# The first output projection's first rows in the joining's free buffer, and the roots behind the first two projections on VectorE

## The chip, the cores and the metric

One core of one Trainium2 chip. The metric is the device time of one launch in microseconds (us), median of several runs; lower is better. The engines are called as the profile calls them: PE (TensorE), DVE (VectorE), ACT (ScalarE), POOL (GpSimd), SP (SyncE, which here only issues transfers).

## What is computed

One decoder layer on a sequence of 2048 rows of 1024 numbers, in float32. `hn` is the row-normed input, `proj` its input projection (q, k, v of an attention group, and the two halves of a gated conv group). What matters here is the middle: the two groups are joined, go through one output projection, and are normed twice.

```python
attn_out = sliding_window_attention(q, k, v, attn_sinks, rel_bias)
conv_out = conformer_conv(u, conv_dw, conv_dw_b, conv_ln_g, conv_ln_b, w_conv_pw)
mixed = jnp.concatenate([attn_out, conv_out], axis=-1) @ w_out
h = h + rms_norm(mixed, mix_post_g)
hn = rms_norm(h, ffn_pre_g)
ff = (jax.nn.silu(hn @ w_gate) * (hn @ w_up)) @ w_down
h = h + rms_norm(ff, ffn_post_g)
```

## The kernel before

The sequence is cut into 4 tiles of 512 rows. Each tile t goes through stages: A (input projection), B (attention), C (31 conv taps on each of four columns of 128 channels, written to `y_scr`, then a tail: load from `y_scr`, transpose, layer norm, swish, store to `mixT`), W (output projection, post norm, residual, second norm). The second norm's rows go to `hn_scr`, from which H transposes them for the feed-forward stages F and G. One extra stage, J, multiplies the conv's pointwise weights into the lower half of `w_out` once (`w_join`), so that the tail's result goes straight into W. H, F and G take two tiles at a time.

Every product is made in three matmuls: each operand is split into a rounded high part and the rest (function `three`, called with PE's line L108). For a row chunk of `mixT` this is `operand`: ACT copies the high part into half of an `hl` tile (L782), DVE subtracts it into the other half (L85 is the line of all DVE arithmetic). For weights it is `split_w` (ACT L133, DVE L85). So a matmul of W waits for: the load of its rows (L804), ACT's copy, DVE's subtraction, and the same for its weights (load L143).

The tags of `t_` name pools of buffers with a fixed count. Those of the change: `wx`, one buffer of 128 x 1024, used by J for its even inputs and by each W for one residual block (L857); `fa`, four of 128 x 512, used by many stages. `mb` is a pool of two, of which one is a spare tile, used by J for its odd inputs and by W1 for its rows.

The order of the work: the code writes a main run of stages (A0 to A3, then W1, F, G) and lanes beside it that get credit with the main run's progress (`run`, `Lane.pump`); W0 runs in a lane beside A3, as do taps, tails and J. From the dependencies and priorities that this gives, a planner sets a fixed order of instructions for each engine before the launch. Each engine then works through its queue in that order and stops at the first instruction whose inputs or buffer are not there; SP's queue of transfers works in the same way.

W0 is `stage_w(0, True, 2, "x", "hl", "fa", mm)`: four groups of two row chunks (gi = 0 to 3); for each, the two halves of 512 output columns, for each half four row blocks, each a chain of 6 matmuls into a `mm` bank. The first group is copied from the bank by ACT (L757), the others are added by DVE. The banks of `mm` are four; A3 and W share them. Behind it stands `norm_w`: squares summed by ACT (L844), a root, scale, residual, squares again (L866), the second root, ACT's scaling of four blocks (L873) and the stores to `hn_scr` (L876).

The root is `rsqrt`: three small DVE instructions for a first guess, then three Newton steps on tiles of 128 x 4. With `beside_taps` a step is four POOL instructions (L159 to L162), without it three DVE instructions:

```python
if beside_taps:
    ptt(t, y, y, ALU.mult)
    ptt(t, t, v, ALU.mult)
    nc.gpsimd.tensor_scalar(t, t, -0.5, 1.5, ALU.mult, ALU.add)
    ptt(y, t, y, ALU.mult)
else:
    vtt(t, y, y, ALU.mult)
    stt(t, v, -0.5, t, ALU.mult, ALU.mult)
    stt(y, t, 1.5, y, ALU.add, ALU.mult)
```

Before, W0, W1 and W2 use POOL, W3 uses DVE.

Of the kernel before, what the change touches and what calls it, by code (L numbers as in the profile page):

```python
# [23 lines left out]
D = 1024  # L24
DFF = 2816
P = 128
T = 512
# [10 lines left out]
def layer_kernel(ctx, tc, x, xT, cols, rows, sinks, relb, onehot, w_in, w_four, w_pw, w_out, w_gate, w_up, w_down, out):  # L38
# [10 lines left out]
    def nm(s):  # L49
        uid[0] += 1  # L50
        return f"{s}@{lab[0]}_{uid[0]}"
# [3 lines left out]
    def t_(tag, shape, dt=F32):  # L55
        return sb.tile(list(shape), dt, tag=tag, name=nm(tag), bufs=BUFS[tag])

    def f4(tag, shape=(P, D)):
        return t_(tag, shape)

    def f2(tag, shape=(P, T)):
        return t_(tag, shape)

    def hl(tag):
        return t_(tag, (P, 2, T), F32R)

    def sm(n, dt=F32):
        kind = "A" if lab[0][0] == "G" else lab[0][0]
        return sb.tile([P, 8], dt, tag="sm" + kind, name=nm("sm"), bufs={"C": 8, "W": 4}.get(kind, 16))[:, 0:n]
# [70 lines left out]
    def weight(src, low, made, raw=None, on_pool=True):  # L140
        if raw is None:
            raw = t_("raw", (P, 2, T))
            nc.sync.dma_start(raw, src)  # L143
        return [split_w(raw[:, n], "w", low[n], made, on_pool) for n in range(2)]
# [5 lines left out]
    def rsqrt(ssq, n, mean_over, beside_taps=True):  # L150
        v = sm(n)
        y = sm(n)
        t = sm(n)
        vts(v, ssq, 1.0 / mean_over, EPS, ALU.mult, ALU.add)
        vts(y.bitcast(I32), v.bitcast(I32), 1, None, ALU.logical_shift_right)
        vts(y.bitcast(I32), y.bitcast(I32), -1, 0x5F3759DF, ALU.mult, ALU.add)
        for _ in range(3):
# [9 lines that stand above are left out]
        return y  # L167
# [453 lines left out]
    def stage_tail(t, sink=None):  # L621
        L = f"C{t}"
        lab[0] = L
        yt = t_("yt", (P, 4, 4 * P))
        ycs = []
        turn = turner(yt, ycs)
        for c in range(4):
            lab[0] = L
            y = f2("fc")
            nc.sync.dma_start(y, y_scr[c, :, t * T : (t + 1) * T])  # L630
            ycs.append(y)
            turn(c)
            yield 0.5
        yield from conv_tail(t, yt, sink)
# [34 lines left out]
    def spare_tile():  # L669
        if not spare:  # L670
            spare.append(t_("mb", (P, 2, T)))
        return spare[0]
# [76 lines left out]
    def block_half(acc, units, n, first, L, bank_of, s0=0):  # L749
        cs = slice(n * T, (n + 1) * T)  # L750
        for i in range(len(acc)):
            s = i + s0
            lab[0] = L
            o = bank_of()
            three(o, [((a[s // 4][:, 0, ss(s)], a[s // 4][:, 1, ss(s)]), (w[:, 0], w[:, 1])) for a, w in units])
            if first:
                act(acc[i][:, cs], o, AF.Copy)  # L757
            else:
                vtt(acc[i][:, cs], acc[i][:, cs], o, ALU.add)
            yield 0.65 * len(units)  # L760

    def load_gb(row):
        gb = []
        for n in range(2):
            t = f2("gb")
            nc.sync.dma_start(t, rows[row, n * T : (n + 1) * T].partition_broadcast(P))
            gb.append(t)
        return gb

    def post_scale(acc, gb, r):  # L770
        for n in range(2):
            cs = slice(n * T, (n + 1) * T)
            tied(stt(acc[:, cs], acc[:, cs], r, gb[n], ALU.mult, ALU.mult))

    def stage_w(w, spill, G, atag, htag, mtag, bank_of, norm=None):
        L = f"W{w}"
        lab[0] = L
        acc = [f4(atag) for _ in range(4)]

        def operand(m):  # L780
            a = hl(htag)
            act(a[:, 0], m, AF.Copy)  # L782
            vtt(a[:, 1], m, a[:, 0].bitcast(F32), ALU.subtract)
            return [a]

        def acts(gi, ms=None):
            return [operand(m) for m in ms or load(gi)]

        conv = []
        tail = stage_tail(w, lambda v: conv.append(operand(v))) if w > 1 else ()  # L790
        for y in tail:
            if y == YL2:
                break
            yield y
        lab[0] = L

        stage = spare_tile() if w == 1 else None

        def load(gi):
            ms = []  # L800
            pair_ = stage if w == 1 else t_("wx", (P, 2, T)) if w > 1 and gi == 0 else None
            for c in range(G * gi, G * gi + G):
                ms.append(pair_[:, c % 2] if pair_ is not None else f2(mtag))
                nc.sync.dma_start(ms[-1], mixT[c, :, w * T : (w + 1) * T])  # L804
            return ms

        first = load(0)
        gb = load_gb(0) if w > 1 else None
        if w != 1:
            yield 5.0 if w == 0 else 8.0  # L810
            lab[0] = L
        nxt = acts(0, first)
        for gi in range(KC // G):
            if w > 1 and G * gi == 4:
                yield from tail
                lab[0] = L
            aa = nxt if w < 2 or G * gi < 4 else conv[G * gi - 4 : G * gi - 4 + G]
            for n in range(2):
                lab[0] = L
                more = gi + 1 < KC // G and (w < 2 or G * gi + G < 4)  # L820
                if n == 0 and more:
                    if w < 2 and G * gi + G == 4:
                        ld.until(f"C{w}")
                        lab[0] = L
                    rows_next = load(gi + 1)
                if n == 1 and more:
                    nxt = acts(gi + 1, rows_next)
                src = w_out[2 * gi : 2 * gi + 2] if gi < 2 else w_join[2 * gi - 4 : 2 * gi - 2]
                ws = weight(src[:, :, n * T : (n + 1) * T].rearrange("c p t -> p c t"),
                            lo_out[n, 2 * gi : 2 * gi + 2], w > 0, on_pool=False)  # L830
                yield from block_half(acc, list(zip(aa, ws)), n, gi == 0, L, bank_of)
        last = norm_w(w, spill, acc, mtag, gb)
        if norm:
            norm(last)
        else:
            yield from last

    def norm_w(w, spill, acc, mtag, gb):
        L = f"W{w}"
        lab[0] = L  # L840
        gb = gb or load_gb(0)
        ssq = sm(4)
        for s in range(4):
            act(junk, acc[s], AF.Square, accum_out=ssq[:, s : s + 1])  # L844
            yield 0.5
            lab[0] = L
        r = rsqrt(ssq, 4, D, w < 3)
        yield 3
        lab[0] = L
        ssq2 = sm(4)  # L850
        for s in range(4):
            lab[0] = L
            post_scale(acc[s], gb, r[:, s : s + 1])
            r0 = w * T + s * P
            if s == (2 if mtag == "fa" else 0):
                xt = f4("wx")
                nc.sync.dma_start(xt, x[r0 : r0 + P])  # L857
                vtt(acc[s], xt, acc[s], ALU.add)
            else:
                for n in range(2):  # L860
                    cs = slice(n * T, (n + 1) * T)
                    xt = f2(mtag if s == 1 or w > 1 else "fa")
                    nc.sync.dma_start(xt, x[r0 : r0 + P, cs])
                    vtt(acc[s][:, cs], xt, acc[s][:, cs], ALU.add)
            nc.sync.dma_start(h_scr[r0 : r0 + P], acc[s])
            act(junk, acc[s], AF.Square, accum_out=ssq2[:, s : s + 1])  # L866
            yield 5.0
        lab[0] = L
        r2 = rsqrt(ssq2, 4, D, w < 3)
        yield 3  # L870
        lab[0] = L
        for s in range(4):
            act(acc[s], acc[s], AF.Copy, scale=r2[:, s : s + 1])  # L873
            if spill:
                r0 = w * T + s * P
                nc.scalar.dma_start(hn_scr[r0 : r0 + P], acc[s])  # L876
        yield 0.1
        hns[w] = acc
# [733 lines left out]
```

## Time and profile before

| | |
|---|---|
| median of 3 runs | 1935.72 us (1932.65 to 1937.01) |
| profiled execution | 1937.05 us, span 1934.7 us |
| mean granted PE clock | 0.993 |
| PE busy | 1897.4 us, 98% |
| DVE busy | 1492.1 us, 77% |
| ACT busy | 970.4 us, 50% |
| POOL busy | 211.5 us, 11% |
| mean DMA rate | 226 GB/s over the span |

In the profile a line of a timeline has the start and the length in us, the engine, the code line, the operation, output and inputs, the count, and in brackets the idle time just before it with what ended it. A line of waits has the total, the count and the longest. A line of windows has the stretch, its length, the busy time of PE, PE's weight loads, DVE, ACT and POOL, the granted PE clock, the DMA share and GB/s. Stages A3, W0 and the taps of C1 and C2 lie between 300 and 470 us, W1 starts at 466 us, F0's first products follow from 534 us.

### The profile page before, as it was taken

To read this page: it belongs to the slowest core of one execution; us is meant where nothing else is said; L and a number is where in the kernel's file an instruction comes from. 1 tells how busy PE (TensorE), PEld (TensorE's weight loads), DVE (VectorE), ACT (ScalarE), POOL (GpSimd) and SP (SyncE) were. 2 spreads that over 40 slices of the span, in tenths; PEclk is the share of its full clock that TensorE was granted. 3 is DMA by queue.
4 is the path that set the end of the run, shared out by engine and by line. 5 is a ranking of instruction groups with operands and counts; after the bars stand their busy time and mean duration, and the time that the engine had idled before them with its cause. 6 is when DMAs were issued, how large, how long until landed. Compare 5 with 4: busy or idle time off the path is not lost.

```text
span 1934.7 us, 26719 instructions
## 1 busy us (share of the span) xinstructions
PE 1897.4 (98%) x8714; PEld 1535.7 (79%) x8714; DVE 1492.1 (77%) x2760; ACT 970.4 (50%) x1911; POOL 211.5 (11%) x311
## 2 busy tenths in 40 slices
PE   9999998999999999999999999999999999999997
PEld 7777776777778878877878878888888888888886
DVE  6999999887876999988988775788566665455557
ACT  5455444656667433433445574676434333345443
POOL 2010012112010000000000010010033333211000
PEclk9999999999999999999999999999999999999999
DMA  9887756669668775787396687699544443376664
GB/s 332 313 279 234 226 171 213 196 229 342 197 239 283 242 249 200 230 279 266 125 320 224 216 308 233 219 346 314 196 166 151 165 151 109 131 240 193 209 193 156
DMA packets 227707, 439.35 MB, mean 227 GB/s; under 512 B 22728, under 2 KB 48752, under 8 KB 227568
## 3 DMA queue, kind: packets, MB, share of 16 engines
q1 hardware_dynamic: 206256, 403.04, 62.6%
q10 hardware_dynamic: 19392, 28.32, 4.1%
q0 software_dynamic: 1920, 6.29, 0.8%
q8 instruction: 68, 1.11, 0.2%
q14 instruction: 71, 0.58, 0.1%
HBM read 318.54 MB, written 119.02 MB: 226 GB/s over the span
## 4 chain that ended last, share of the span: by engine, by line
PE 67%; DVE 16%; DMA 11%; issue 3%; ACT 1%; POOL 1%; SPq 0%; DVEq 0%; ACTq 0%; POOLq 0%
PE mm@F L108 35%; PE mm@G L108 18%; DVE fc@C L85 7%; PE tr@W L108 4%; PE mm@A L108 4%; PE mm@W L108 3%; PE tr@B L108 1%; DMA glu@C<-glu_scr 1%; DVE w@F L85 1%; DMA mids<-fa@F 1%; DMA chl@F<-w_gate 1%; DVE fa@F L85 1%; DVE p@B L493 1%; DMA wx@G<-w_down 1%; DMA fa@G<-mids 1%
## 5 line engine op out<-in xcount | busy, mean ns | idle before, releaser
L85 DVE SCALAR_TENSOR_TENSOR fc@C<-glu@C,colt,fc@C 128x512 f32<-128x512 f32 x480 | 353.3, 753 | 1.9
L108 PE MATMUL mm@F<-hl@H,w@F 128*128 128x512 f32 x1056 | 254.6, 390 | 0.1
L108 PEld LDWEIGHTS mm@F<-hl@H,w@F 128*128 128x128 f32 x1056 | 197.8, 188 | 42.0 <-ACT gb@F L1143 0.9
L108 PE MATMUL mm@G<-hl@G,hl@G 128*128 128x512 f32 x924 | 226.8, 395 | 3.7 <-ACT hl@G L888 3.0
L108 PEld LDWEIGHTS mm@G<-hl@G,hl@G 128*128 128x128 f32 x924 | 171.5, 189 | 41.6 <-ACT hl@G L888 3.8
L888 ACT ACTIVATE w@F<-chl@F 128x512 fp32r<-128x512 f32 x220 | 135.3, 625 | 130.1 <-PE mm@F L108 124.7
L108 PE MATMUL mm@G<-w@G,hl@G 128*128 128x512 f32 x876 | 199.5, 389 | 0.0
L108 PE MATMUL mm@A<-hl@A,w@A 128*128 128x512 f32 x792 | 192.1, 393 | 1.4 <-DVE w@A L85 1.1
L108 PEld LDWEIGHTS mm@G<-w@G,hl@G 128*128 128x128 f32 x876 | 164.4, 188 | 34.1
L108 PEld LDWEIGHTS mm@A<-hl@A,w@A 128*128 128x128 f32 x792 | 147.0, 188 | 34.6 <-issue 1.7
L85 DVE TENSOR_TENSOR w@F<-chl@F,w@F 128x512 fp32r<-128x512 f32 x198 | 144.2, 732 | 35.3 <-ACT w@F L888 34.9
L108 PE MATMUL mm@F<-mid@H,w@F 128*128 128x512 f32 x528 | 131.3, 392 | 3.5 <-DVE fa@F L85 3.5
L108 PE MATMUL mm@F<-ql@H,w@F 128*128 128x512 f32 x528 | 130.5, 391 | 4.3 <-ACT w@F L888 3.3
L108 PE MATMUL mm@F<-p@H,w@F 128*128 128x512 f32 x528 | 129.0, 389 | 0.0
L108 PE MATMUL mm@F<-x@H,w@F 128*128 128x512 f32 x528 | 128.3, 391 | 0.0
L108 PEld LDWEIGHTS mm@F<-mid@H,w@F 128*128 128x128 f32 x528 | 99.4, 189 | 25.1 <-DVE fa@F L85 4.4
L108 PEld LDWEIGHTS mm@F<-ql@H,w@F 128*128 128x128 f32 x528 | 98.4, 188 | 25.7 <-ACT w@F L888 4.1
L108 PEld LDWEIGHTS mm@F<-x@H,w@F 128*128 128x128 f32 x528 | 98.5, 188 | 21.9 <-ACT w@F L888 0.8
L108 PEld LDWEIGHTS mm@F<-p@H,w@F 128*128 128x128 f32 x528 | 99.0, 188 | 20.7 <-ACT at@F L1146 0.2
L108 PE MATMUL mm@W<-w@W,hl@W 128*128 128x512 f32 x384 | 102.0, 411 | 8.2 <-ACT hl@W L782 5.1
L85 DVE TENSOR_TENSOR w@G<-raw@G,w@G 128x512 fp32r<-128x512 f32 x73 | 51.3, 703 | 67.0 <-ACT w@G L888 66.0
L133 ACT ACTIVATE w@A<-raw@A 128x512 fp32r<-128x512 f32 x104 | 63.0, 624 | 64.6 <-DMA raw@A<-w_in 36.5
(314 smaller groups left out, 3197.7 us busy)
## 6 DMA issues: line engine op xcount, KB each, us to landing
mids<-fa@F SPq DMA_DIRECT2D x154, 256.0 KB, 2.8
raw@A<-w_in SPq DMA_DIRECT2D x52, 512.0 KB, 5.3
w@A<-lo_in SPq DMA_DIRECT2D x84, 256.0 KB, 4.7
fc@G<-mids SPq DMA_DIRECT2D x77, 256.0 KB, 3.5
fa@G<-mids SPq DMA_DIRECT2D x75, 256.0 KB, 4.6
w@W<-lo_out SPq DMA_DIRECT2D x48, 256.0 KB, 3.8
chl@F<-w_gate SPq DMA_DIRECT2D x22, 512.0 KB, 4.0
raw@F<-w_gate SPq DMA_DIRECT2D x22, 512.0 KB, 3.8
```

The costliest lines, as they stand in the source:

```text
L85: r = op(*args, **kw)
L108: r = nc.tensor.matmul(*args, **kw)
L133: act(w[:, 0], raw, AF.Copy)
L493: read = nc.vector.tensor_tensor_reduce(out=pr[:, h], in0=os[g][:, j, P:], in1=bias[0][:, h], op0=ALU.add, op1=ALU.max, scale=1.0, scalar=NEG,
L888: act(w[:, 0], x, AF.Copy)
```

## The change

Two edits. The first row group of W0 (gi = 0) takes one `wx` buffer for its two chunks, where it took two `fa` buffers; W2 and W3 did so already, W1 uses the spare tile as before. And both roots of W0 and of W1 take the DVE form; W2 keeps POOL.

```diff
-            pair_ = stage if w == 1 else t_("wx", (P, 2, T)) if w > 1 and gi == 0 else None
+            pair_ = stage if w == 1 else t_("wx", (P, 2, T)) if gi == 0 else None
...
-        r = rsqrt(ssq, 4, D, w < 3)
+        r = rsqrt(ssq, 4, D, w == 2)
...
-        r2 = rsqrt(ssq2, 4, D, w < 3)
+        r2 = rsqrt(ssq2, 4, D, w == 2)
```

That is four roots: 48 POOL instructions less, 36 small DVE instructions more. The planner's order changes with it, between the end of A2 and the middle of F0; from there on it is the same. Three places:

SP's queue while A3 begins, before. `y_scr<-fc@C` stores a conv column after its last tap, `fa@W..<-mixT` are the rows of W0:

```order
L132 DMA w@A_573_3525<-lo_in 128x512
L143 DMA raw@A_609_3700<-w_in 128x1024
L618 DMA y_scr<-fc@C_420_2645 128x512
L593 DMA glu@C_544_3397<-glu_scr 128x542
L804 DMA fa@W_561_3488<-mixT 128x512
L804 DMA fa@W_562_3490<-mixT 128x512
L383 DMA glu_scr<-fa@A_550_3441 128x512
L804 DMA fa@W_565_3498<-mixT 128x512
```

The same place now:

```order
L132 DMA w@A_572_3524<-lo_in 128x512
L143 DMA raw@A_608_3699<-w_in 128x1024
L804 DMA fa@W_564_3497<-mixT 128x512
L804 DMA fa@W_565_3499<-mixT 128x512
L618 DMA y_scr<-fc@C_420_2645 128x512
L593 DMA glu@C_544_3397<-glu_scr 128x542
L383 DMA glu_scr<-fa@A_550_3441 128x512
L132 DMA w@A_609_3701<-lo_in 128x512
```

The two `fa` loads that now stand ahead of the store are W0's second group. Its first group, `L804 DMA wx@W_561_3488<-mixT 128x512 x2`, has moved some fifty rows forward, to where `L857 DMA wx@W<-x` stood during A2; that one stands a few rows ahead of the piece shown.

PE's queue at the same time, one piece of the difference (`tr@B_535` and `tr@B_534` are attention scores of tile 2, `mm@A_573` or `574` is a unit of A3; the first of the twelve score matmuls stands for all, and the piece goes on behind them):

```order
 L108 MATMUL mm@A_549_3416<-hl@A_524_3276,w@A_548_3413 128x512 x3
+L108 MATMUL mm@W_569_3511<-w@W_567_3503,hl@W_562_3491 128x512
+L108 MATMUL mm@A_573_3527<-mid@A_503_3142,w@A_571_3521 128x512 x3
+L108 MATMUL mm@A_573_3527<-mid@A_504_3146,w@A_571_3521 128x512 x3
+L108 MATMUL mm@A_573_3527<-mid@A_505_3150,w@A_571_3521 128x512 x3
+L108 MATMUL mm@W_569_3511<-w@W_567_3503,hl@W_562_3491 128x512
+L108 MATMUL mm@A_573_3527<-mid@A_506_3154,w@A_571_3521 128x512
+L108 MATMUL mm@W_569_3511<-w@W_567_3503,hl@W_562_3491 128x512
 L108 MATMUL tr@B_535_3338<-kz,ql@A_493_3093 128x256
```

W0's first matmul stood behind the twelve scores, ahead of the A3 unit; now it and most of that unit's first half stand ahead of the scores. Further on, the first transpose of C1's tail (`ct@C1`, L602) stands behind 24 more matmuls of A3, one more of W0 and four more 128 x 128 ones, counted from the end of A2.

ACT's queue where W1 begins, before (`hl@W_850` and `851` are W1's second row group, `ql@A` a q copy of A3, `x@W` the blocks of W0's second norm, `mid@W` W1's sums):

```order
L873 ACTIVATE x@W_558_3485<-x@W_558_3485,sm@W_777_4666 128x1024
L873 ACTIVATE x@W_559_3486<-x@W_559_3486,sm@W_777_4666 128x1024
L782 ACTIVATE hl@W_850_5101<-mb@J_341_2174 128x512
L873 ACTIVATE x@W_560_3487<-x@W_560_3487,sm@W_777_4666 128x1024
L876 DMA hn_scr<-x@W_557_3484 128x1024
L782 ACTIVATE hl@W_851_5104<-mb@J_341_2174 128x512
L876 DMA hn_scr<-x@W_558_3485 128x1024
L445 ACTIVATE ql@A_789_4769<-mm@A_787_4737 128x512
L133 ACTIVATE w@W_838_5030<-raw@W_837_5028 128x512
L133 ACTIVATE w@W_839_5033<-raw@W_837_5028 128x512
L876 DMA hn_scr<-x@W_559_3486 128x1024
L757 ACTIVATE mid@W_790_4782<-mm@W_799_4804 128x512
```

The same place now:

```order
L782 ACTIVATE hl@W_849_5094<-mb@J_341_2174 128x512
L782 ACTIVATE hl@W_850_5097<-mb@J_341_2174 128x512
L445 ACTIVATE ql@A_788_4762<-mm@A_786_4730 128x512
L133 ACTIVATE w@W_837_5023<-raw@W_836_5021 128x512
L133 ACTIVATE w@W_838_5026<-raw@W_836_5021 128x512
L757 ACTIVATE mid@W_789_4775<-mm@W_798_4797 128x512
L873 ACTIVATE x@W_557_3484<-x@W_557_3484,sm@W_776_4662 128x1024
L873 ACTIVATE x@W_558_3485<-x@W_558_3485,sm@W_776_4662 128x1024
L873 ACTIVATE x@W_559_3486<-x@W_559_3486,sm@W_776_4662 128x1024
L873 ACTIVATE x@W_560_3487<-x@W_560_3487,sm@W_776_4662 128x1024
L876 DMA hn_scr<-x@W_557_3484 128x1024
L757 ACTIVATE mid@W_790_4776<-mm@W_813_4887 128x512
```

The copy of W1's first bank (L757) and what stood ahead of it were behind the scalings of W0; now the four scalings stand between the first and the second copy. On DVE the second root's nine instructions stand between eight taps of C2, and their last three among two subtractions of `hl@W`, the copy `vtok` (L437), a q subtraction and two copies `vd`.

## The prediction

> **What bounds the kernel now.** I read the busy shares first, then PE's list of waits, then the engines' timelines around the three longest waits in the stretch that the change touches.
>
> ```profile
> span 1934.7 us, 26719 instructions
> PE 1897.4 (98%) x8714; PEld 1535.7 (79%) x8714; DVE 1492.1 (77%) x2760; ACT 970.4 (50%) x1911; POOL 211.5 (11%) x311
> PE mm@W L108 <- ACT hl@W L782: 5.1, 1, 5.1
> PE ct@C L602 <- DMA fc@C<-y_scr: 2.9, 2, 2.5
> PE mm@W L108 <- ACT mid@W L757: 2.8, 1, 2.8
> ```
>
> PE is the bound: it idles 1934.7 - 1897.4 = 37.3 us. No matmul goes away, so the change can only act on that idle time and on matmuls that run at a low clock after a wait. The last three lines (total, times, longest) are the candidates: two waits in W0 and W1, and one for the conv's rows. The time of this execution is 1937.05 us, 2.35 around its span; the median of the runs, 1935.72, is 1.33 lower.
>
> **Stall 1, the part with wx.** W0's first matmul waits for the split of its rows:
>
> ```profile
> 327.40 0.80 PE L108 MATMUL mm@W<-w@W,hl@W 128*128 128x512 f32 x1 [5.08 <-ACT hl@W L782]
> 327.99 3.48 PE L108 MATMUL mm@A<-mid@A,w@A 128*128 128x512 f32 x9
> 331.31 0.39 PE L108 MATMUL mm@W<-w@W,hl@W 128*128 128x512 f32 x1
> 331.54 0.84 PE L108 MATMUL mm@A<-mid@A,w@A 128*128 128x512 f32 x3
> 332.22 1.07 PE L108 MATMUL mm@A<-hl@A,w@A 128*128 128x512 f32 x4
> 326.72 1.27 ACT L782 ACTIVATE hl@W<-fa@W 128x512 fp32r<-128x512 f32 x2 [3.91 <-DMA fa@W<-mixT]
> 321.99 0.32 SPq L618 DMA_DIRECT2D y_scr<-fc@C  x1
> 322.83 0.93 SPq L804 DMA_DIRECT2D fa@W<-mixT  x2
> SPq L618 <- DVE fc@C L85: 13.1, 3, 6.3
> 198.72 0.33 SPq L857 DMA_DIRECT2D wx@W<-x  x1
> 300.00:320.00 20.00, 20.00 (x105) 15.15 (x104) 19.96 (x34) 9.46 (x17) 5.12 (x4) 1.00 0.76 245
> 328.00:330.00 2.00, 2.00 (x6) 1.63 (x5) 2.00 (x6) 0.00 (x0) 0.00 (x0) 0.50 0.88 161
> ```
>
> The rows' load (322.83) stood in SP's queue behind the store of a conv column (L618), which waited up to 6.3 us for DVE's last tap. Then the load, ACT's copy, and PE. After the wait the granted clock (third number from the end of the window's row) is 0.50. At full rate three matmuls take 332.22 - 331.54 = 0.68, so 0.227 each; the eleven from 327.40 to 331.54 took 4.14 instead of 2.50. Stall 1 costs 5.08 + 1.64 = **6.7 us**.
>
> After, these rows go to wx. Their two loads stand in SP's queue where the residual's load of wx stood (198.72), behind the same release, over 120 us ahead of need. The two ACT copies stand among instructions that ran near 305 us; in the row of 300 to 320 ACT is busy 9.46 of 20, DVE 19.96. The two DVE subtractions follow, 2 x 0.6 us of DVE work that moves forward and does not grow. The residual's load of wx moves behind these subtractions, to about 308 us, over 100 us before the norm needs it. The second pair of rows moves ahead of the store, too. So the whole wait goes. What is late next is the conv.
>
> **Stall 2, what catches it.**
>
> ```profile
> 380.27 0.63 PE L602 MATMUL ct@C<-ident,fc@C 128*128 128x128 f32 x4 [2.49 <-DMA fc@C<-y_scr]
> 371.28 0.32 SPq L618 DMA_DIRECT2D y_scr<-fc@C  x1
> 372.13 0.43 SPq L663 DMA_DIRECT2D mixT<-fc@C  x1
> 373.73 0.32 SPq L630 DMA_DIRECT2D fc@C<-y_scr  x1
> 331.98 0.69 DVE L85 TENSOR_TENSOR hl@W<-fa@W,hl@W 128x512 fp32r<-128x512 f32 x1 [0.74 <-ACT hl@W L782]
> 334.52 0.69 DVE L85 TENSOR_TENSOR hl@W<-fa@W,hl@W 128x512 fp32r<-128x512 f32 x1 [1.04 <-ACT hl@W L782]
> ```
>
> C1's last column is stored when DVE's last tap is done (371.28), and the load issued at 373.73 lands when PE goes on at 380.27, after 2.49 us. This chain is DVE's. In the new order PE has 24 more matmuls of A3, one of W0 and four small ones ahead of this transpose, about 27 x 0.227 = 6.1 us. If the conv's rows came no sooner than now, PE would reach the transpose at 380.27 - 2.49 - 6.7 + 6.1 = 377.2 and wait 3.1 us, with 6.1 us more done: a gain of 6.1, or 3.4 if that wait cools the clock (I price this by the next stall, 2.7 to 3.1). If they came 3.1 sooner, the gain would be 6.7 + 2.5 = 9.2. DVE loses the waits of 0.74 and 1.04, and an hl subtraction and three adds (0.6 each) move behind the last tap, 4.2 us together; but the new load stands behind the store of C0's last column, and these four stand ahead of that. I take a gain of **7.5** at this point, from 3.4 to 9.2.
>
> **Stall 3, the part with the roots.**
>
> ```profile
> 438.61 0.19 POOL L159 TENSOR_TENSOR sm@W<-sm@W 128x4 f32<-128x4 f32 x1 [20.90 <-DVE sm@W L85]
> 442.08 0.20 POOL L162 TENSOR_TENSOR sm@W<-sm@W,sm@W 128x4 f32<-128x4 f32 x1
> 460.56 0.62 POOL L159 TENSOR_TENSOR sm@W<-sm@W 128x4 f32<-128x4 f32 x1 [15.32 <-DVE sm@W L85]
> 467.10 0.20 POOL L162 TENSOR_TENSOR sm@W<-sm@W,sm@W 128x4 f32<-128x4 f32 x1
> 467.33 2.19 ACT L873 ACTIVATE x@W<-x@W,sm@W 128x1024 f32<-128x1024 f32 x2 [5.43 <-POOL sm@W L162]
> 474.70 7.25 PE L108 MATMUL mm@W<-w@W,hl@W 128*128 128x512 f32 x18 [2.81 <-ACT mid@W L757]
> 481.88 0.98 PE L108 MATMUL tr@B<-kz,ql@A 64*128 64x256 f32 x12
> 476.00:478.00 2.00, 2.00 (x6) 1.52 (x6) 1.55 (x4) 0.97 (x2) 0.00 (x0) 0.50 0.96 332
> L85 DVE SCALAR_TENSOR_TENSOR sm@W<-sm@W,sm@W x12: 152/156/167, 1229.1 to 1277.4; 128x4 f32<-128x4 f32 x12
> 442.35 0.69 DVE L85 SCALAR_TENSOR_TENSOR ql@A<-mm@A,ql@A 128x512 fp32r<-128x512 f32 x1 [2.38 <-ACT ql@A L445]
> 466.67 0.69 DVE L437 COPY vtok<-mm@A 128x512 f32<-128x512 f32 x1 [0.83 <-PE mm@A L434]
> ```
>
> W0's second root ends on POOL at 467.30; ACT idles 5.43 for it, scales four row blocks (about 1.1 each), and only then copies W1's first bank (L757); PE waits 2.81. The 18 matmuls from 474.70 to 481.88 took 7.18 instead of 18 x 0.227 = 4.09. Stall 3 costs 2.81 + 3.1 = **5.9**.
>
> The first root, 3.7 us on POOL from 438.61, becomes nine DVE instructions of 0.156, about 1.4 us. It gains nothing: behind it DVE waits until 442.35 for ACT's q copy anyway, and three of the nine now stand behind that, at most +0.4. The second is spread between eight taps, and its last steps stand behind the copy of v (466.67), another q subtraction (0.6) and two copies of a quarter of v (0.5 at most): with two small instructions 466.67 + 0.69 + 0.6 + 0.5 + 0.25 = 468.7 on the old clock, 1.4 us later than POOL. But ACT's new order has W1's row splits and the first bank's copy ahead of the four scalings. So PE gets a fourth group of 6 matmuls, to 471.9 + 1.4 = 473.3, and the second bank is free at 468.7 + 4 x 1.1 + 0.5 = 473.6. The wait would be 0.3 and the clock might hold: a gain of up to 5.6. Against that stands the DMA, full while W1's weights come:
>
> ```profile
> 440.00:460.00 20.00, 20.00 (x94) 15.23 (x94) 17.65 (x28) 12.84 (x23) 3.46 (x11) 1.00 0.99 357
> 460.00:480.00 20.00, 17.19 (x75) 13.39 (x74) 12.29 (x28) 11.14 (x17) 5.84 (x12) 0.85 1.00 359
> ```
>
> (Its share is the last but one number.) A PE that runs on uses weights sooner than they may land. Nearest row for such a wait: 2.81. I take **3.0**, from -2 (a root 5 us later than worked out, in front of the second bank's copy) to 5.6. Scaling 1.4 us later delays H0's input: 0 to 1.4, I take 0.5. W1's two roots, 18 DVE instructions of 0.156 or 2.8 us, come beside F0's first products; the list of PE's waits has none for W's sums, so I price them at nothing, and at 2.8 if PE should wait for DVE there.
>
> The sum: 1937.05 - 7.5 - 3.0 + 0.5 = **1927.05 us**; its ends are 1937.05 - 9.2 - 5.6 = 1922.3 and 1937.05 - 3.4 + 2 + 1.4 + 2.8 = 1939.9.
>
> **A rule on the clock.** The clock was 0.50 after the wait of 2.81, above, and this is the row of the wait of 2.49:
>
> ```profile
> 380.00:382.00 2.00, 1.73 (x12) 1.60 (x13) 2.00 (x5) 0.41 (x1) 0.00 (x0) 1.00 1.04 414
> ```
>
> So between waits of 2.5 and 2.8 us the price doubles here, and I have counted it so. [...]
>
> **The rivals.**
>
> *The slow clock of stall 3 stays.* The wait shrinks, the 3.1 us of low clock do not: the gain there is 2.5 less 0.5 for H0 and the first bank's split, 1937.05 - 7.5 - 2 = 1927.6 at best, and 1930 with only the certain 6.1 and half of the wait. For it: 2.81 lies near 2.49, which cost nothing. Chance 0.08.
>
> *The wait only moves.* Stall 1 goes, DVE's taps and the conv's loads hold PE for 3.1 us with a cold clock, and W1's start waits for weights as long as it waited for its bank: 1937.05 - 3.4 = 1933.7, up to 1937 if the conv's rows come 3 us later still. For it: C1's chain is DVE's, and DVE has no gap from 300 to 320. Against: DVE idles 0.74 and 1.04 behind the very rows that now come early. That only one of the two edits acts lies here, too: the first alone gives 1929.5 to 1933.7, the second alone 1931.5 to 1937. Chance 0.22.
>
> *Slower: DVE cannot follow between 442 and 467.* From 442.35 to 466.67 it idles only 0.83 in 24 us, and the change adds 18 instructions. If the 2.38 that ended at 442.35 is set by ACT and not by PE's lead, PE arrives 7.5 us early at the v and q of A3, waits there, and starts cold: the 7.5 are lost, 3.1 of slow clock and 18 x 0.156 = 2.8 of DVE work come on top: 1937.05 + 5.9 = 1943. It decides from the point at which ACT's queue has less than 7.5 us to give. Against:
>
> ```profile
> 386.82 0.70 DVE L85 TENSOR_TENSOR w@W<-raw@W,w@W 128x512 fp32r<-128x512 f32 x1 [1.04 <-ACT w@W L133]
> 439.28 0.69 DVE L85 SCALAR_TENSOR_TENSOR fc@C<-fc@C,fc@C 128x512 f32<-128x512 f32 x1 [0.76 <-ACT fc@C L658]
> 447.77 0.60 ACT L445 ACTIVATE ql@A<-mm@A 128x512 fp32r<-128x512 f32 x1 [2.10 <-PE mm@A L108]
> ```
>
> The first two are the first and last of nine DVE waits between 381 and 442, 9.2 us in all, each for ACT or PE; and ACT's next q copy waits 2.10 for PE, so ACT has room. Chance 0.18.
>
> **How the numbers follow.** Forecast 0.52, the others as above. The forecast's own range is 1922 to 1932; the others add 1927 to 1937 and 1943. With 1920 to 1940, the slow end of the last rival and little else is left out. A measurement here can tell about 0.2%, 3.9 us, from no change: faster is under 1931.9. That gives faster 0.60 (forecast and the clock's rival), same 0.22, slower 0.18.
>
> **What would show it.** The line of PE's waits for hl@W behind L782 is gone or under 0.5; the L804 loads of wx stand near 199 us; ct@C of C1 still waits 0 to 3 us; the wait for mid@W is under 1 and the clock after it is 1.00; ACT's idle time before L873 ends on DVE, not POOL; POOL has 48 fewer instructions. Wrong would make it: a PE wait over 3 us for ql@A, vtok or w@W between 440 and 500, or a new slow-clock stretch after ct@C.

## The result, and the profile after

The changed kernel took 1927.77 us (median of 7 runs, 1923.48 to 1930.63), the kernel before 1937.01 (median of 7 beside them, 1932.65 to 1944.71). The ratio is 0.9946, 95% interval 0.993 to 0.9962. Run again later on another 11 executions it was 0.9956 (0.9942 to 0.9971). So it is faster by about 0.5%, 8 to 10 us (the two intervals together leave 5.6 to 13.6); 1927.0 was forecast. The total came out right. Its parts did not, and most of what follows is about that.

The profiled execution of the changed kernel took 1926.44 us. Its page begins:

```profile
span 1924.7 us, 26694 instructions
PE 1891.3 (98%) x8714; PEld 1531.9 (80%) x8714; DVE 1492.3 (78%) x2796; ACT 970.1 (50%) x1911; POOL 197.0 (10%) x263
```

The list of PE's waits of the changed kernel (what for, us in total, times, longest):

```profile
PE ct@C L602 <- DMA fc@C<-y_scr: 3.9, 2, 2.8
PE mm@G L108 <- ACT hl@G L888: 3.8, 2, 3.1
PE tr@B L535 <- DVE sm@B L493: 2.1, 2, 1.5
PE mm@W L108 <- DVE hl@W L85: 1.6, 1, 1.6
PE mm@W L108 <- ACT mid@W L757: 1.3, 1, 1.3
PE mm@W L108 <- ACT x@W L757: 0.8, 1, 0.8
```

The wait of 5.08 for `hl@W` behind L782 has left the head of the list, and the wait for `mid@W` at W1's start fell from 2.81 to 1.3. But new ones stand beside them: for `x@W`, for the softmax's sums `sm@B`, for `hl@W` behind DVE. PE's timeline of the changed stretch shows where (last in the brackets is what ended the wait):

```profile
336.65 1.66 PE L108 MATMUL mm@W<-w@W,hl@W 128*128 128x512 f32 x6 [0.75 <-ACT x@W L757]
353.31 0.66 PE L535 MATMUL tr@B<-ident,p@B 128*128 128x128 f32 x4 [1.50 <-DVE sm@B L493]
381.70 1.11 PE L602 MATMUL ct@C<-ident,fc@C 128*128 128x128 f32 x4 [2.78 <-DMA fc@C<-y_scr]
394.34 0.66 PE L602 MATMUL ct@C<-ident,fc@C 128*128 128x128 f32 x4 [0.56 <-ACT yt@C L603]
408.87 0.63 PE L535 MATMUL tr@B<-ident,p@B 128*128 128x128 f32 x4 [0.65 <-DVE sm@B L493]
464.06 0.60 PE L434 MATMUL mm@A<-ident,fa@A 128*128 128x128 f32 x4
474.89 5.74 PE L108 MATMUL mm@W<-w@W,hl@W 128*128 128x512 f32 x24 [1.25 <-ACT mid@W L757]
511.95 2.13 PE L108 MATMUL mm@W<-w@W,hl@W 128*128 128x512 f32 x8 [0.48 <-ACT hl@W L782]
516.51 3.02 PE L108 MATMUL mm@W<-w@W,hl@W 128*128 128x512 f32 x12 [1.55 <-DVE hl@W L85]
```

The waits shown for the changed kernel between 320 and 520 us make 9.5 us; those of the kernel before in the same stretch, added up from the same view, made 11.8. Idle time there fell by 2.3 us. What fell besides is the length of the single wait, and with it, in this execution, the time at a low clock. In the kernel before, the clock was at 0.50 after stalls 1 and 3, which cost 1.6 and 3.1 us. In the changed kernel it is low in one place of that stretch, at a cost of 1.5 us, behind the 2.78 us for C1's rows (columns: us, PE, PEld, DVE, ACT and POOL busy, granted clock, DMA share, GB/s):

```profile
380.00:382.00 2.00, 0.30 (x2) 0.31 (x3) 2.00 (x11) 0.00 (x0) 0.04 (x1) 0.82 0.86 258
382.00:384.00 2.00, 2.00 (x8) 1.71 (x7) 2.00 (x6) 1.86 (x10) 0.00 (x0) 0.50 0.86 256
384.00:386.00 2.00, 2.00 (x9) 1.61 (x8) 1.93 (x5) 2.00 (x11) 0.00 (x0) 0.83 0.92 299
```

To compare two executions place by place, I took the start times of the same matmul rows in both, and set them against each other from the row at 278.40 us of before, where both kernels still do the same. This is the row of before at A3's end, to be set against 464.06 above:

```profile
466.04 0.60 PE L434 MATMUL mm@A<-ident,fa@A 128*128 128x128 f32 x4
```

Of 10.2 us that the first pair of profiles differs by, 2.5 are won there (464.06 in an execution that was 0.5 us late at 278.40), 4.8 at 617 us, and 5.2 more between 617 and 973 us, in F0, which the change does not touch and in which PE's matmuls stand in the same order in both. Whether that last half belongs to the change is the first thing to test.

### The profile page after: what moved, and what is told of

Read it like the earlier page. It is cut to its first block, busy times and chain, and to the rows that moved or that the text cites. A ratio compares the mean times of both kernels' runs of the same rounds, so it can differ in the third digit from the quotient of the medians.

```text
span 1924.7 us, 26694 instructions
## 1 busy us (share of the span) xinstructions
PE 1891.3 (98%) x8714; PEld 1531.9 (80%) x8714; DVE 1492.3 (78%) x2796; ACT 970.1 (50%) x1911; POOL 197.0 (10%) x263
## 4 chain that ended last, share of the span: by engine, by line
PE 75%; DMA 11%; DVE 9%; issue 2%; ACT 1%; SPq 1%; POOL 0%; DVEq 0%; ACTq 0%; POOLq 0%
PE mm@F L108 36%; PE mm@G L108 20%; PE mm@A L108 9%; PE tr@W L108 4%; DVE fc@C L85 2%; PE tr@B L108 2%; PE mm@W L108 2%; PE ct@J L108 1%; DMA hl@A<-x 1%; DVE chl@F L85 1%; DVE w@F L85 1%; DMA mids<-fa@F 1%; DMA td<-fc@G 1%; DMA chl@F<-w_gate 1%; DMA wx@G<-w_down 1%
```

## The experiments

The tables give the median, the ratio to the kernel before with its 95% interval, and the mean granted clock of the timed runs. The clock of the kernel before was 0.993 in every group.

| kernel | runs | median us | ratio | clock |
|---|---|---|---|---|
| the change | 7 | 1927.8 | 0.9946 (0.993 to 0.9962) | 0.9961 |
| the change again | 11 | 1927.9 | 0.9956 (0.9942 to 0.9971) | 0.9964 |
| before again | 10 | 1936.7 | 1.0 (0.9988 to 1.0013) | 0.9927 |
| first edit alone | 7 | 1927.6 | 0.9954 (0.9937 to 0.9971) | 0.9966 |
| second edit alone | 11 | 1930.5 | 0.997 (0.9955 to 0.9984) | 0.9942 |
| both, W1's roots on POOL | 7 | 1929.0 | 0.996 (0.9944 to 0.9976) | 0.9963 |
| before, first rows by POOL's queue | 12 | 1935.7 | 0.9994 (0.998 to 1.0008) | 0.9941 |
| the change, C1's first load by POOL | 6 | 1927.0 | 0.9959 (0.9943 to 0.9975) | 0.9967 |
| second edit, first rows by POOL | 12 | 1930.0 | 0.9967 (0.9952 to 0.9983) | 0.9958 |
| before, second root of W0 on DVE | 11 | 1931.3 | 0.9973 (0.996 to 0.9985) | 0.9951 |
| first edit and second root of W0 | 9 | 1924.9 | 0.9946 (0.9929 to 0.9964) | 0.9967 |
| the change with a filler in G0 | 12 | 1932.0 | 0.9984 (0.9972 to 0.9996) | 0.9968 |

**The kernel before, again.** No edit.

> The kernel before, unchanged, profiled a second time. Theory (the gain is the changed stretch up to H0 plus something that recurs): the waits of 5.08 for hl@W near 321 us and 2.81 for mid@W near 475 come back to within 0.3 us, and so do the waits of F0 between 623 and 974 us (0.86 to 2.67 each, about 8 us together), so that PE again needs about 5 us more from 623 to 974 us than the changed kernel. Rival (F0's 5 us are a draw of one execution): the first two waits come back, F0's do not, and the span is about 1929 to 1931.

Stalls 1 and 3 came back (4.8 and 3.2 us). The waits of F0 did not all: the list of PE's waits from 617 to 975 us, first of the kernel before in its first profile, then in its second.

```profile
PE mm@F L108 <- DVE fa@F L85: 3.5, 2, 2.7
PE mm@F L108 <- ACT w@F L888: 3.3, 2, 2.1
PE mm@F L108 <- ACT mm@F L1132: 1.0, 1, 1.0
```

```profile
PE mm@F L108 <- ACT w@F L888: 2.6, 2, 2.3
PE mm@F L108 <- DVE gb@F L85: 1.3, 1, 1.3
PE mm@F L108 <- DVE fa@F L85: 1.2, 1, 1.2
```

The same kernel was at the same point at 617 us (0.04 us apart) and 4.7 us earlier at 973 us. In between it had 2.5 us less of waits and no low clock, where the first profile had 1.7 us lost behind the wait of 2.67. The rival holds: F0's 5 us are a draw of one execution. One pair of profiles cannot be read to better than that. Five profiles with the changed kernel's order of PE up to G0 (the change twice and three variants) were 4.8, 0.5, 5.1, 5.3 and 5.6 us ahead at 617 us, 4.2 in the mean.

**Each edit alone.** The first:

```diff
-            pair_ = stage if w == 1 else t_("wx", (P, 2, T)) if w > 1 and gi == 0 else None
+            pair_ = stage if w == 1 else t_("wx", (P, 2, T)) if gi == 0 else None
```

> Only the first edit: the first rows of W0 in wx; all roots of W0 and W1 stay on GpSimd. Theory: PE's wait of 5.08 for hl@W near 321 us is gone, the wait for C1's rows stays at 2.5 to 3.1, ScalarE still scales W0's four row blocks ahead of the copy of W1's first bank, so W1's start still waits 2 to 5 us for mid@W with a clock near 0.5 after it: 1930 to 1934 us, ratio 0.996 to 0.998. Rival (the two edits are worth nothing apart, the wait only moves on to W1's start): ratio 0.999 to 1.001.

It brings as much as both together. Its PE waits:

```profile
337.27 1.65 PE L108 MATMUL mm@W<-w@W,hl@W 128*128 128x512 f32 x6 [1.69 <-ACT x@W L757]
380.55 0.66 PE L602 MATMUL ct@C<-ident,fc@C 128*128 128x128 f32 x4 [1.06 <-DMA fc@C<-y_scr]
470.39 4.41 PE L108 MATMUL mm@W<-w@W,hl@W 128*128 128x512 f32 x18 [1.69 <-DVE ql@A L85]
```

No wait from 320 to 500 is over 1.8 us, the clock is 1.00 from 466 to 482, and the 18 matmuls of W1 from 470.39 take 4.41 us, not the 7.25 of before. I had said that ACT's four scalings ahead of W1's first bank would keep stall 3 at 2 to 5 us. That was wrong. W0 ran sooner, and POOL finished its second root at 465.35, not 467.30; and in the order that comes with early rows ACT has W1's two row splits (L782) ahead of the scalings, at 461.00, where before they stood between and behind them, at 470.47 and 472.03. The second edit alone:

```diff
-        r = rsqrt(ssq, 4, D, w < 3)
+        r = rsqrt(ssq, 4, D, w == 2)
...
-        r2 = rsqrt(ssq2, 4, D, w < 3)
+        r2 = rsqrt(ssq2, 4, D, w == 2)
```

> Only the second edit: the roots of W0 and W1 on VectorE; the first rows of W0 stay in fa. The planner's order differs from that of both kernels. Theory: the wait of 5.08 for hl@W stays; ScalarE's order still has the four scalings ahead of W1's first bank, so the wait at W1's start stays at 1 to 4 us: 1934 to 1938 us, ratio 0.999 to 1.001. Rival (the faster root alone brings stall 3's gain): the wait at W1's start is under 1 us with a full clock, ratio 0.996 to 0.998.

It brings two thirds as much, and by the rival's way: stall 3 is gone (the stretch at W1's start, PE busy throughout), stall 1 is not.

```profile
460.00:480.00 20.00, 20.00 (x111) 15.44 (x110) 13.90 (x44) 16.35 (x38) 0.00 (x0) 1.00 1.03 367
```

```profile
325.41 0.80 PE L108 MATMUL mm@W<-w@W,hl@W 128*128 128x512 f32 x1 [3.57 <-ACT hl@W L782]
```

So either edit removes most of stall 3, and only one of the two can be paid for it.

**Which of the roots.** Two variants: both edits but W1's two roots back on POOL (`w in (1, 2)` in place of `w == 2` in both calls); and the kernel before with only W0's second root on DVE:

```diff
-        r2 = rsqrt(ssq2, 4, D, w < 3)
+        r2 = rsqrt(ssq2, 4, D, w in (1, 2))
```

> Both edits, but W1's two roots back on GpSimd; PE's order is that of the changed kernel row by row and ScalarE's in all but two. Theory (the order, and W0's roots, carry the gain; W1's roots are worth nothing): within 0.1% of the changed kernel, 1926 to 1930 us, ratio 0.9945 to 0.9965. Rival (W1's roots on VectorE bring the 5 us of F0, since the roots lie beside F0's first products): 1931 to 1934 us, ratio 0.997 to 0.999, with PE's waits in F0 as in the kernel before.

> The kernel before with only the second root of W0 on VectorE; the other three roots stay on GpSimd. TensorE's order is that of before up to W1's end. Theory (stall 3 is the late second root: 6.7 us on GpSimd beside VectorE's taps): ScalarE's first scaling begins near 463, not 467.3, the wait for mid@W falls from 2.8 to 3.2 to under 1 us with a clock of 1.00 after it; stall 1 stays at about 5: 3 to 5 us won by 500 us, 1931 to 1934 us, ratio 0.997 to 0.9985. Rival (VectorE, full beside the taps, finishes the root no sooner): the scaling begins at 466 or later, the wait stays over 2 us, ratio 0.9985 to 1.001.

W1's roots are worth nothing that can be measured (0.996 against 0.9946 and 0.9956, the intervals overlap). W0's second root is the one that counts. By itself it won 5.1 us between A3's end and 617 us in its profile. ACT's four scalings, which began at 467.33 before, in this variant:

```profile
465.40 4.26 ACT L873 ACTIVATE x@W<-x@W,sm@W 128x1024 f32<-128x1024 f32 x4
```

On DVE the root takes from 459.12 to 465.0, twelve small instructions spread between taps; before, its first guess began on DVE at 458.67 and POOL's steps ran from 460.56 to 467.30. The scalings begin 1.9 us sooner, not the 4 that I expected. PE has no wait at W1's start and a clock of 1.00 from 460 to 500 us. The root's time is not all of that: PE's order is the old one only up to the stall, ACT's only up to these scalings. W1's two row splits now stand ahead of them, and PE has twelve scores (`tr@B`) ahead of the matmuls that waited. The first copy of a W1 bank came at 471.08, where it had been 474.07. Of these 3.0 us, 1.9 are the scalings' earlier start, and the rest lies in ACT's order.

**Why the first rows were late, and what they are worth.** The kernel before with the two loads of W0's first rows issued by POOL, still into `fa`; nothing else moves on PE, DVE and ACT.

```diff
-                nc.sync.dma_start(ms[-1], mixT[c, :, w * T : (w + 1) * T])
+                (nc.gpsimd if w + gi == 0 else nc.sync).dma_start(ms[-1], mixT[c, :, w * T : (w + 1) * T])
```

> The kernel before with nothing changed but the queue of W0's two first row loads: issued by GpSimd, not SyncE; they still go into fa, and the rows of TensorE, VectorE and ScalarE are those of the kernel before, one by one. Theory (the loads were late because they stood in SyncE's queue behind the store of a conv column, which waits for VectorE's last tap): the loads are issued near 312 us, not 322.8, the wait of 4.8 to 5.1 for hl@W is under 1 us, the clock from 320 to 332 is 1.00; 6 to 8 us are won there, of which a longer wait for C1's rows may take back 1 to 3: 1929 to 1933 us, ratio 0.996 to 0.998. Rival (fa's buffers come free late, so that only the other buffer helps): the loads are issued after 320 us on GpSimd too, the wait is 4 to 5, ratio 0.999 to 1.001.

This is the most telling run, though it moves only half of what the first edit moves. First POOL's issue of the loads, then PE's waits.

```profile
311.46 1.08 POOL L804 DMA_DIRECT2D fa@W<-mixT  x2
```

```profile
323.55 0.50 PE L108 MATMUL mm@W<-w@W,hl@W 128*128 128x512 f32 x1 [1.06 <-ACT hl@W L782]
335.02 2.34 PE L108 MATMUL mm@W<-w@W,hl@W 128*128 128x512 f32 x9 [1.39 <-ACT fa@A L376]
339.20 1.66 PE L108 MATMUL mm@W<-w@W,hl@W 128*128 128x512 f32 x6 [1.84 <-ACT x@W L757]
341.77 0.33 PE L654 MATMUL ct@C<-ident,yt@C 128*128 128x128 f32 x1 [0.91 <-ACT yt@C L650]
```

The loads went out at 311.5, not 322.8, so `fa` was free and SyncE's queue had held them. Stall 1 fell from 5 us to 1.06 with a clock of 1.00 from 320 to 360 us. Against the second profile of before, set equal at 278.40, PE was 5.9 us ahead at 333 us. At 345 us it was 0.1 ahead: it had run into ACT's copies of the banks and of `yt`. The measured time is that of the kernel before (0.9994; the interval leaves a gain of at most 3.9 us). Neither of my two theories had this: stall 1 was not worth its price, because ACT's queue held PE some 12 us later anyway. (At 617 us this profile was again 4.1 us ahead of both profiles of before. Against the first of them, 2.6 of that came at W1's start, where a wait of 3.07 happened to keep the clock, 1.00 from 468 to 484 us.)

ACT itself was held by the second pair of W0's rows, whose loads this run leaves where they were (the last line is from SP's list of waits, 305 to 345 us):

```profile
331.22 0.63 ACT L782 ACTIVATE hl@W<-fa@W 128x512 fp32r<-128x512 f32 x1 [7.20 <-DMA fa@W<-mixT]
333.85 0.63 ACT L782 ACTIVATE hl@W<-fa@W 128x512 fp32r<-128x512 f32 x1 [1.48 <-DMA fa@W<-mixT]
SPq L804 <- DMA glu_scr<-fa@A: 1.7, 1, 1.7
```

They went out at 326.23 and 329.37 (326.06 and 329.63 before), behind the same store at 322.16, and the second of them waited 1.7 us more for a buffer of `fa`. ACT then worked without a gap from 333.85 to its copy of the bank (L757 at 338.57), and this ended PE's wait of 1.84. In the changed kernel the first pair takes none of the four `fa` buffers, the second pair's loads stand ahead of the store, and both are issued at 316.18 to 317.22; ACT's copies follow:

```profile
322.52 1.28 ACT L782 ACTIVATE hl@W<-fa@W 128x512 fp32r<-128x512 f32 x2 [0.26 <-DMA fa@W<-mixT]
```

So the first edit brings two things that this run lacks: the second pair of rows some 10 us sooner, and the order that the planner makes of early rows. No run has one without the other, and which of them is worth more stays open. The order puts 24 matmuls of A3 into the gap (the rows from 338.76 of the first edit alone):

```profile
338.76 2.88 PE L108 MATMUL mm@A<-mid@A,w@A 128*128 128x512 f32 x12
341.49 2.88 PE L108 MATMUL mm@A<-hl@A,w@A 128*128 128x512 f32 x12
344.20 0.62 PE L108 MATMUL mm@W<-w@W,hl@W 128*128 128x512 f32 x2
```

The same edit on top of the second edit alone:

> The second edit alone (roots on VectorE, first rows of W0 in fa) with W0's two first row loads issued by GpSimd; the rows of the other three engines are those of the second edit alone. Theory (the second edit alone has no stall at W1's start, so taking stall 1 away by the queue adds its whole price of 3.6 us of wait and 3.4 us of slow clock): the wait for hl@W under 1, mid@W under 0.5, full clock to 540 us; 5 to 7 us less than the second edit alone: 1923 to 1926 us, ratio 0.992 to 0.995, and so a little faster than the changed kernel. Rival (the two gains overlap, as they do in the changed kernel): the wait at W1's start or for C1's rows comes back, 1927 to 1930 us.

It brought nothing either (0.9967 against 0.997): stall 1's wait fell to 1.05, and 1.43 and 1.85 came back at 337 and 341, behind the same waits of ACT for the second pair (7.22 and 1.48).

**What holds C1's rows in the changed kernel.** The load of C1's first column issued by POOL, so that it does not stand behind the store of C0's last column:

```diff
-            nc.sync.dma_start(y, y_scr[c, :, t * T : (t + 1) * T])
+            (nc.gpsimd if t == 1 and c == 0 else nc.sync).dma_start(y, y_scr[c, :, t * T : (t + 1) * T])
```

> The changed kernel with one DMA moved: the load of C1's first column is issued by GpSimd, not SyncE, so that it does not stand behind the store of C0's last column; the rows of TensorE, VectorE and ScalarE are those of the changed kernel. Theory (the wait of 2.78 for C1's rows is that queue's, and the slow clock after it is the wait's): the wait is under 0.5, the clock from 380 to 390 is 1.00, 2.8 + 1.7 = 4.5 us are won by 394 us: 1922 to 1925 us, ratio 0.991 to 0.994. Rival (C1's chain is VectorE's): the wait goes but comes back at the next transposes of C1 or at the softmax, within 40 us: 1926 to 1929 us.

The load on POOL's queue, with what ended POOL's idle time, and then ACT's last copy for C0's last column:

```profile
377.33 0.55 POOL L630 DMA_DIRECT2D fc@C<-y_scr  x1 [8.02 <-DVE fc@C L85]
```

```profile
375.53 0.78 ACT L658 ACTIVATE fc@C<-ct@C,colt 128x512 f32<-128x512 f32 x1 [3.12 <-DMA y_scr<-fc@C]
```

The theory fell. On its own queue the load went out at 377.33, against 376.98 in the changed kernel, and PE still waited 2.12. The load waits for its buffer: DVE frees it when it has used the tanh of C0's last column, and ACT could not give it the other half (L658) before the store of C1's column from a third buffer had landed. All three buffers of `fc` are in that chain. A fourth was not tried. Here the clock held after 2.12 us (1.00 from 374 to 392), and the time was that of the changed kernel.

**The two working parts together**, the first edit and W0's second root:

> The first edit and only the second root of W0 on VectorE; its first root and both of W1 stay on GpSimd. Theory (both working parts of the change are in it, but they overlap, since the first edit alone already left 1.7 us of wait and a full clock at W1's start): as the changed kernel and the first edit alone, 1925 to 1929 us, ratio 0.994 to 0.997, the wait for mid@W under 1.5 with a full clock. Rival (the gains add): the first edit's 9 and the second root's 5 to 6 make 14, 1921 to 1923 us.

1924.9 us, ratio 0.9946: the gains overlap, as the theory had it. Its profile has no wait for `mid@W`. It has the lowest median of all, but its interval holds the ratios of the change and of the first edit alone.

**The change again, and a filler.** The control, and 26 transposes of the identity at G0's start.

```diff
-            ah, al = a[:, 0, ss(b)], a[:, 1, ss(b)]
+            ah, al = a[:, 0, ss(b)], a[:, 1, ss(b)]; [nc.tensor.transpose(banks[0][:, 0:P], ident, ident) for _ in range(26 if ws[0] == 0 and i == 0 and b == 0 else 0)]
```

> The changed kernel once more, as a control. Theory (of the gain some 6 us are full clock time that waits over 2.4 us took in the kernel before, the rest idle time): mean time 1926 to 1929 us, mean granted clock 0.996 to 0.997 against 0.993 for the kernel before, so that the time less the share of slow clock differs by only 2 to 3 us between the two kernels; in its profile each piece of lost clock is 1.7 or 3.4 us and stands within some microseconds of a PE wait of over 1.4 us. Rival (the clock is as low in both, the gain is idle time alone): clock 0.993 to 0.995.

> The changed kernel with 26 needless transposes of the identity matrix (0.09 us each, about 2.3 us) at the start of G0, written into the PSUM bank that its first product then starts afresh; TensorE waits there for 2.4 to 3.6 us in all ten profiles so far, and nine of them show a lower clock behind it. The order of the other matmuls stays up to G0 and shifts a little behind it. Theory (it is the idle TensorE that lowers the clock): the wait shrinks to under 1.5 us, the clock from 980 to 1000 us is 1.00, 1.5 to 2 us won: 1924 to 1927 us. Rival (the clock falls for another reason, such as the load of DMA and the other engines): clock under 0.9 there as often as not, no gain, or a loss of up to 2 us by the needless work.

The control shows how much one kernel varies. W1's start in this execution, and the clock around it:

```profile
477.15 7.35 PE L108 MATMUL mm@W<-w@W,hl@W 128*128 128x512 f32 x24 [2.08 <-ACT mid@W L757]
```

```profile
476.00:478.00 2.00, 0.85 (x4) 0.72 (x5) 2.00 (x10) 2.00 (x5) 0.00 (x0) 1.00 1.04 392
478.00:480.00 2.00, 2.00 (x7) 1.50 (x6) 0.49 (x4) 2.00 (x6) 0.00 (x0) 0.52 1.01 395
480.00:482.00 2.00, 2.00 (x7) 1.63 (x6) 0.00 (x0) 2.00 (x13) 0.00 (x0) 0.62 1.04 413
```

A wait of 2.08 instead of 1.25, and the same 24 matmuls take 7.35 us instead of 5.74. The filler failed as a test: its transposes stand 20 us ahead of the wait that they should fill (966.83 and 988.86), and the order behind G0 is another. The wait was 1.29 with a clock of 1.00 from 980 to 1000 us, but the kernel is 4 us slower than the changed one. That the low clock comes of an idle PE is thus shown only by where it stands, in or behind a wait of at least 1.85 us in all 33 cases of the last section, not by a run that takes the idle time alone away.

## Why the prediction was right in its sum and wrong in its terms

*Stalls 1 and 2, taken at 7.5 (3.4 to 9.2): 2.5 measured at A3's end, below the range* (0.8, 2.3, 2.6 and 3.2 in the four other profiles with this order of PE). This is the step that failed. Stall 1 did go: at 333 us PE was 7.0 us ahead. My 7.5 lies between conv rows that come no sooner and rows that come 3.1 us sooner. They came 0.9 us later than before (381.70, less the 0.5 by which this execution was late, against 380.27; in the four other profiles 0.2 to 2.3 later). PE waited 2.78 for them, with 1.5 us of low clock behind it, and then 0.56 and 0.65 more for `yt` and for the softmax's sums. From the 6.1 us of work that I had PE do ahead of the rows, that leaves 6.1 - 0.9 - 1.5 - 1.2 = 2.5. The run with C1's load on POOL's queue shows what made the rows late, a buffer and not the queue, and the changed kernel has the same row:

```profile
375.05 0.78 ACT L658 ACTIVATE fc@C<-ct@C,colt 128x512 f32<-128x512 f32 x1 [4.20 <-DMA y_scr<-fc@C]
```

Before, this copy ran at 370.52, ahead of the store of C1's last column (371.28). Now that store is issued at 367.96, and the copy waits for it to land. I had DVE's taps and the load's place in the queue in the sum, and no wait for a buffer. Two more waits that I had not seen, for ACT's copy of W0's first banks (0.75; 1.9 to 2.1 in three others of this order) and for the softmax's sums (1.50), come ahead of this one. In this profile they cost nothing by themselves, since without them PE would have stood longer at C1's rows, unless they delayed the rows; no run settles that. The low clock behind `ct@C` is one of the signs of being wrong that I had named. The loads of the rows into `wx` stood at 207.45, not near 199, and nothing hung on that.

*Stall 3, taken at 3.0: about 2.4 measured* between L434 and F0's first product, new waits of 0.48 and 1.55 for `hl@W` included (3.0, 2.9 and 2.5 in three of the other profiles, nothing in the control, whose wait of 2.08 cost it the clock). The wait was 1.25, not 0.3, since ACT's queue stood for W1's weights, not for the root:

```profile
468.56 1.15 ACT L133 ACTIVATE w@W<-raw@W 128x512 fp32r<-128x512 f32 x2 [3.71 <-DMA raw@W<-w_out]
469.62 0.57 ACT L757 ACTIVATE mid@W<-mm@W 128x512 f32<-128x512 f32 x1
470.10 2.18 ACT L873 ACTIVATE x@W<-x@W,sm@W 128x1024 f32<-128x1024 f32 x2
```

ACT's idle time ahead of the scalings, which I said would end on DVE, ended on a DMA; the scalings began 0.9 us after the root was done on DVE (469.19). Late weights were the reason for which I took 3.0 and not 5.6. H0's later input, put at 0.5, cannot be told from the two new waits. By the variant, the second root, with the order that comes with it, is worth 5.1, near the 5.9 of stall 3; the first edit had taken most of that already.

*The first edit alone at 1929.5 to 1933.7, the second at 1931.5 to 1937:* measured 1927.6 and 1930.5. Both are better than I said, and they do not add.

*W1's roots at nothing:* right. *Slower, because DVE cannot follow:* it did not happen; the wait for `ql@A` in the first edit alone was 1.69.

*What filled the sum.* The first pair of profiles differs by 5.2 us in F0, which the control shows to be chance. That the timed runs still differ by 8 to 10 us is largely the clock. The close fit of the total is luck: the two places gave 4.2 us in the mean of five profiles, not the 10.0 that I had added up, and the execution that I counted from, 1937.05, happened to equal the median beside the result (1937.01; later medians of the same kernel were 1935.3 to 1936.5). Over the runs of the control's group the mean time was 1936.0 before (25 runs) and 1927.6 after (11), the mean clock 0.9928 and 0.9964. Time that a low clock can cost is one less the clock, times the time: 13.9 and 7.0 us. This counts low clock during a wait too, which costs nothing (1.8 and 0.7 us of it in stall 1 in the two profiles of before), so 5 to 6 of the 8.4 us are clock. I had counted 1.6 and 3.1 for it at two places and saw the doubling as tied to the size of a wait. Of the 42 waits of 2.0 to 3.3 us in the 13 profiles 26 were followed by a loss (last section), so at this length it is a matter of odds, and by the mean clock the change moved the odds. The rest of the 8.4 beyond the 4.2 must lie behind the changed stretch, where chance moves each profile by several us; these few profiles do not fix its place, and it stays open.

## What to carry to other kernels

A wait that an engine ends is worth its price only if nobody else is late a little behind it; ask for the next 20 us of every queue that the waiting engine draws on, and expect that two edits that both let one engine run ahead are paid once. When a load is taken out of a queue, look at the next one behind the same store. A long wait cut into several short ones may be a gain without less idle time: of the waits under 2 us here one in 55 was followed by a low clock, of the longer ones 32 in 48. No run here shows that gain alone. Before reading a place by place comparison, profile the unchanged kernel twice: here the control moved 4.7 us in a stretch that nobody had touched.

## What the hardware showed that I had not expected

The loss of clock comes in pieces. I took all PE waits of at least 1 us of the 13 profiles (past the first 20 us) and summed one less the clock over the 14 us from each wait's start. Every sum was 0, 1.7 or 3.4 us:

| wait of PE, us | waits | with a loss | each |
|---|---|---|---|
| 1.0 to 2.0 | 55 | 1, of 1.85 | 1.7 |
| 2.0 to 2.4 | 19 | 9 | 1.7 |
| 2.4 to 3.3 | 23 | 17 | 1.7, once 3.4 |
| 3.5 to 5.1 | 6 | 6 | 3.4 |

(In the first line two are not counted as having a loss: a wait of 1.09, whose loss belongs to one 8 us behind it, and one of 1.43, whose loss belongs to the 1.85 some 4 us behind it.) A wait of 2.49 us for C1's rows kept the clock and one of 2.51 at the same place, in the same kernel, lost it.

The clock records of the traces show where a loss falls. Without the first 20 and the last 30 us, the 13 executions have 33 low pieces, all at a granted clock of 0.50: 26 of 3.41 us, which lose 1.7 each, and seven of 6.83, which lose 3.4. Within each trace the starts of the low pieces lie whole numbers of 3.413 us apart (44, 114 and 40 of them in the first profile of before). I divided each execution into steps of 3.413 us from these starts and added up PE's idle time in each. In the 33 steps at full clock that were followed by a low one, PE idled 1.84 to 3.41 us. In the 7067 others at full clock it idled 1.87 us at most. So in these traces a low piece came behind every step with more than 1.87 us of idle time and behind none with less than 1.84, and a wait of 2 to 3.3 us had that much in one step or lay across two. The wait of 2.49 had 1.81 us in one step, the 2.51 lay whole in one. What sets the steps no run here shows.

As an estimate from the table, these waits can be priced at 0.8 us each (9 of 19 times 1.7) from 2.0 to 2.4, at 1.3 to 3.3 (18 pieces of 1.7 in 23), and at 3.4 above 3.5; the part that falls into the wait itself is free (1.8 of the 3.4 in stall 1 of the first profile of before).
